# Accumulators of an input projection as tiles of one PSUM bank

## The chip, the cores and the metric

The kernel runs on one core of a Trainium2 chip. The metric is device time in microseconds of that core, from a whole execution. The engines are TensorE (PE in the profile, with PEld for its weight loads), VectorE (DVE), ScalarE (ACT), GpSimd (POOL) and SyncE (SP), whose queue issues most transfers. Each engine runs its own instructions in order and waits for the others by semaphores. TensorE adds its results up in PSUM, which this kernel uses as eight banks of 128 x 512 fp32.

## The reference

One encoder layer, applied with the same weights to two sequences of 512 tokens, D_MODEL = 1024, all fp32:

```python
h = rms_norm(x, norm_g)
proj = jnp.einsum('bsd,de->bse', h, w_in)
c_q, c_kv, k_rope, gate_a, conv_in, gate_c, mg_a, mg_c = split_columns(proj)
...                                     # latent attention with 8 heads
y_a = jnp.einsum('bse,ed->bsd', attn * jax.nn.silu(gate_a), w_o_attn)
u = conv_in[..., :CONV_WIDTH] * jax.nn.sigmoid(conv_in[..., CONV_WIDTH:])
...                                     # depthwise conv over 31 positions, + bias
u = jax.nn.silu(layer_norm(u, conv_ln_g, conv_ln_b)) * jax.nn.silu(gate_c)
y_c = jnp.einsum('bsc,cd->bsd', u, w_pw2)
merged = jax.nn.sigmoid(mg_a) * y_a + jax.nn.sigmoid(mg_c) * y_c
return x + jnp.einsum('bsd,de->bse', merged, w_out)
```

The change lies in `proj`, in those of its column blocks that feed the gates and the convolution, and in the LayerNorm and swish behind the convolution.

## The kernel before

Everything is computed channels first: a column block of the projection is 128 output channels by 1024 tokens (two sequences, "b" 0 and 1, of 512), that is two PSUM banks. Each fp32 matmul is made of three at higher pace: inputs and weights are split into a rounded part (hi) and the rest (lo), and hi\*hi, lo\*hi and hi\*lo are summed. ACT makes hi (L128 for plain weights, L178 for combined ones), POOL or DVE makes lo (L129, L179).

**The start.** The tokens are normalised and transposed on PE (`trans_x`, L275), read out of PSUM by ACT and DVE (`evac_x`, L306 and L307), and for the second sequence combined (`combine_x`, L290 to L299, with POOL). Meanwhile blk0 and blk1, the first two column blocks, are accumulated (L452, L461). blk0 is the gate half of the GLU's first pair (a "cb"), blk1 the value half ("ca").

**The streamed projection.** `plan` lists what follows: a *single* (L341) is one column block, 48 matmuls of 128x512 in the rows named blki (L325). A *seven* (L359) computes two column blocks together by a Strassen scheme with seven products instead of eight: each product (L351, matmuls at L355 to L357) is 12 matmuls into one bank. The seven's four banks are a and c, which are px (blkx in the profile), and d and b, which are py_ (blky). Its order on PE is a, b, d, b again, c, a again, d again, 84 matmuls. Between the products other engines work on the banks: ACT copies a (L372) and b (L375), POOL subtracts the copies (u2, L376), DVE makes v (L382), b = d - v (L383), c = c + v (L387) and d = d - u2 (L394). Combined weights for a seven come from sums on POOL (L147 to L158). There are 10 singles and 11 sevens from the first single (a cb) to the end of the last seven; twelve more singles follow, and the last six of them are the tail, in which `tokens` is interleaved.

**The readers.** `take` (L481) hands each finished pair of banks on: a cb goes through a sigmoid on ACT (L484), a ca is multiplied with it on DVE (u, L490), and gates go through an activation and to memory (`gate_out`, L476 and L477). From each u DVE computes the convolution, 30 taps of 128x1024 in a chain (L412), eight u's in all, each stored when done (y_s, L414). `drain` puts these taps between the products.

**Behind it.** `tokens` loads y back by tokens (L527), transposes it on PE (yT, L533), normalises it (L538 to L543), transposes again (zT, L549) and applies swish (L552 to L556), between the matmuls of the last singles. Then come the projection w_pw2 (`block`), attention, and w_out.

**PSUM.** Pool pp has three tiles of two banks [P, 2, S], for the column blocks, for px and py_, and for zT; p1 has two banks for x transposes, which py, the accumulator of the convolution, takes afterwards, and then yT. A matmul into a tile waits for an earlier reader or writer of the same tile.

**The order of the work.** PE's instructions in the projection stand in the order in which they are written (`manual_schedule`); the other engines' order is set ahead of time by a scheduler that goes by estimated times and the priorities given in the code. So an edit can move rows on engines that the text of the edit doesn't mention.

Of the kernel before, what the change touches and what calls it, by code (L numbers as in the profile page):

```python
# [9 lines left out]
F32 = mybir.dt.float32  # L10
# [33 lines left out]
def encoder_block(tc, xp_d, xs_d, win_d, wkr_d, whd_d, wqr_d, wo_d, wp_d, wout_d, vec_d, dwk_d, rg_d, rc_d, yp_d, ys_d):  # L44
# [275 lines left out]
    def block_mm(ps, i, xh, xl, grp, ks=range(KD)):  # L320
        whi, wlo = (w.rearrange("p (k c) -> p k c", k=KD) for w in wdone[i])
        for k in ks:
            for wl_, xl_, b in SEQ:
                if b in grp:
                    mm(  # L325
                        ps[:, b],
                        (wlo if wl_ else whi)[:, k],
                        xl(k, b) if xl_ else xh(k, b),
                        start=(k == 0 and wl_ == 0 and xl_ == 0),
                        stop=(k == KD - 1 and wl_ == 1),  # L330
                    )
# [6 lines left out]

    used = [0]

    def single(between=lambda: None):  # L341
        e = used[0]
        ensure(e + 3)
        ps = fresh(f"i{e}")
        block_mm(ps, stream[e][0], hh, hl, (0, 1), ks=range(4))
        between()
        block_mm(ps, stream[e][0], hh, hl, (0, 1), ks=range(4, KD))
        used[0] += 1
        return flat(ps)

# [8 lines left out]
    def seven(emit):  # L359

        e = used[0]
        px, py_ = fresh(f"x{e}"), fresh(f"y{e}")
        a, c, d, b = px[:, 0], px[:, 1], py_[:, 0], py_[:, 1]
        quad = lambda kk, bb: lambda k: (hH[4 * kk + k, bb], hL[4 * kk + k, bb])
# [25 lines left out]
        ensure(e + 6)  # L390
        emit(0, flat(px))
        product(d, e + 3, 0, comb(4), False)
# [3 lines left out]
        drain(3)  # L396
        emit(1, flat(py_))

# [67 lines left out]
    DVE.tensor_mul(gqk, vec[:, V_GQ : V_GQ + 1], vec[:, V_GK : V_GK + 1])  # L466
    close_pool("x", "p1")
    py = open_pool("py", bufs=1, space=PSUM)
# [4 lines left out]

    def gate_out(nm, j, pool, tag, ps):
        st = pool.tile([P, NT], F32, tag=tag, name=f"st{nm}{j}")
        ACT(st, ps, AF.Silu if nm[0] == "g" else AF.Sigmoid)  # L476
        nc.scalar.dma_start(spill[nm][j], st)  # L477

    sigs = {}

    def take(nm, j, ps):  # L481
        if nm == "cb":
            sigs[j] = cv.tile([P, NT], F32, tag="sig", name=f"sig{j}", bufs=1)
            ACT(sigs[j], ps, AF.Sigmoid)  # L484
        elif nm == "ca":
# [3 lines left out]
            with tc.high_priority(offset=100):  # L489
                DVE.tensor_mul(u[:, :, PAD : PAD + S], half(ps), half(sigs[j]))  # L490
            waiting.append(conv_ops(j, u))
        else:
            gate_out(nm, j, sp, "s", ps)

    take("cb", 0, flat(first[0]))
    take("ca", 0, flat(first[1]))
    with tc.manual_schedule(engines={nc.tensor.engine}):
# [48 lines left out]
    def swish(i, z):  # L546
        ps = pp.tile([P, KD, P], F32, tag="pp", name=f"zT{i}")
        for j in range(KD):
            nc.tensor.transpose(ps[:, j], z[:, j * P : (j + 1) * P], identf)  # L549
        zs = zp.tile([P, KD, P], F32, tag="zs", name=f"zs{i}")  # L550
        for j in range(KD):
            ACT(zs[:, j], ps[:, j], AF.Silu, scale=vec[:, V_LG + j : V_LG + j + 1], bias=vec[:, V_LB + j : V_LB + j + 1])  # L552
        DVE.tensor_mul(zs, zs, stok[i])
# [21 lines left out]
    for i in range(4):  # L575
        nc.gpsimd.tensor_mul(rt[:, i], rc[:, i % 2], rg[:, i].unsqueeze(1).to_broadcast([P, 4, RD]))
    close_pool("z", "s", "w1", "ln")
    wp = open_pool("w", bufs=2, side="left")
# [21 lines left out]
    close_pool("m", "c")  # L600
    p1 = open_pool("p1", bufs=2, space=PSUM)

# [528 lines left out]
```

## Time and profile before

| | |
|---|---|
| Median of 3 runs | 1210.38 us (1209.24 to 1213.36) |
| Profiled execution, its own time | 1211.43 us |
| Its span, first to last instruction | 1209.6 us |
| Mean granted TensorE clock | 0.994 |
| First matmul of a single (blki) between the x transposes | 29.87 us |
| First matmul of the first seven | 96.02 us |
| End of the last seven | 411.55 us |
| First transpose of `tokens` on PE | 487.71 us |

The profile names instructions by engine, source line, operation, and tile out<-in. A row of a timeline gives start and length in us, and in brackets how long the engine was idle ahead of it and what released it. Matmuls overlap, so that rows of 0.39 us follow each other at 0.23. A line of waits gives the engine and tile that waited, what it waited for, then total us, count, and the longest. SPq is SP issuing a transfer.

### The profile page before, as it was taken

The page shows a single profiled execution, that of the slowest core. Times are in us where ns is not written, and L with a number is a line of the kernel's source. Part 1 is how long each engine was busy: PE and PEld are TensorE (multiplying, and loading weights), DVE is VectorE, ACT ScalarE, POOL GpSimd, SP SyncE. Part 2 cuts the span into 40 slices and gives each one's busy share as a digit, 9 for nine tenths or more (in the row PEclk, how much of TensorE's full clock was granted, in tenths as well). Part 3 has the DMA queues.
Part 4 walks back from the last instruction along what each step waited for, and adds up shares of the span by engine and source line. Part 5 has one row for each costly group of instructions (what it writes and reads, how often), then busy time and mean ns, then how long its engine had stood idle before and what let it go on. Part 6 is the DMA issues. An engine that isn't in the chain of part 4 may idle for free.

```text
span 1209.6 us, 14998 instructions
## 1 busy us (share of the span) xinstructions
PE 1152.1 (95%) x5856; PEld 967.3 (80%) x5856; DVE 764.7 (63%) x1104; ACT 484.9 (40%) x871; POOL 343.4 (28%) x292
## 2 busy tenths in 40 slices
PE   7999989988988999999999999999999999999998
PEld 5677767767766788887888888799999998888887
DVE  5599999899999900573121345678778889343411
ACT  6532234233234221674011233766767687111200
POOL 5864565566466332210000001222221221000000
PEclk9999999999999999999999999999999999999999
DMA  6022212213213363453444011111001101234531
GB/s 248 1 71 87 87 53 106 87 53 105 87 53 114 130 204 105 132 152 117 157 156 139 28 47 60 62 34 34 25 19 34 33 30 39 85 132 160 186 105 70
DMA packets 46518, 109.51 MB, mean 91 GB/s; under 512 B 3696, under 2 KB 20336, under 8 KB 46448
## 3 DMA queue, kind: packets, MB, share of 16 engines
q1 hardware_dynamic: 41552, 91.78, 23.0%
q10 hardware_dynamic: 4896, 16.78, 3.6%
q8 instruction: 46, 0.75, 0.3%
q14 instruction: 24, 0.20, 0.0%
HBM read 79.18 MB, written 29.36 MB: 90 GB/s over the span
## 4 chain that ended last, share of the span: by engine, by line
PE 60%; DVE 5%; ACT 3%; issue 1%; POOL 1%; ACTq 0%; DVEq 0%; POOLq 0%
PE blk L325 21%; PE blki L325 8%; PE po L1053 7%; DVE py L412 3%; PE pt L820 2%; PE pkv L728 1%; PE pkv L730 1%; PE pkv L729 1%; PE av L830 1%; PE av L831 1%; PE av L832 1%; PE sc L801 1%; PE sc L803 1%; PE sc L802 1%; PE sc L804 1%
## 5 line engine op out<-in xcount | busy, mean ns | idle before, releaser
L412 DVE SCALAR_TENSOR_TENSOR py<-u,dwk,py 128x1024 f32<-128x1024 f32 x224 | 288.4, 1288 | 6.3
L128 ACT CAST whi<-raw 128x1024 fp32r<-128x1024 f32 (+3 forms) x59 | 60.5, 1025 | 300.9 <-PE blk L325 165.4
L325 PE MATMUL blki<-hH,whi 128*128 128x512 f32 x352 | 138.0, 392 | 1.7 <-ACT sig L484 1.7
L325 PE MATMUL blki<-hL,whi 128*128 128x512 f32 x352 | 137.1, 389 | 0.0
L325 PE MATMUL blki<-hH,wlo 128*128 128x512 f32 x352 | 108.5, 390 | 0.5 <-DVE wlo L129 0.5
L129 DVE TENSOR_TENSOR wlo<-raw,whi 128x1024 fp32r<-128x1024 f32 (+2 forms) x38 | 54.5, 1434 | 56.3 <-ACT whi L128 56.2
L355 PE MATMUL blky<-tH,ohi 128*128 128x512 f32 x176 | 69.8, 397 | 12.7 <-ACT u L375 12.7
L179 POOL TENSOR_TENSOR olo<-s,ohi 128x512 fp32r<-128x512 f32 x44 | 57.5, 1318 | 77.2 <-ACT ohi L178 77.2
L325 PEld LDWEIGHTS blki<-hH,whi 128*128 128x128 f32 x352 | 66.1, 188 | 15.6 <-ACT sig L484 2.1
L325 PEld LDWEIGHTS blki<-hH,wlo 128*128 128x128 f32 x352 | 66.0, 188 | 14.8 <-DVE wlo L129 0.9
L325 PEld LDWEIGHTS blki<-hL,whi 128*128 128x128 f32 x352 | 66.1, 188 | 13.4
L129 POOL TENSOR_TENSOR wlo<-raw,whi 128x1024 fp32r<-128x1024 f32 x20 | 48.2, 2412 | 82.5 <-ACT whi L128 82.5
L355 PE MATMUL blkx<-hH,ohi 128*128 128x512 f32 x132 | 54.1, 410 | 18.1 <-DVE blkx L387 18.1
L356 PE MATMUL blky<-tL,ohi 128*128 128x512 f32 x176 | 68.7, 390 | 0.0
L357 PE MATMUL blky<-tH,olo 128*128 128x512 f32 x176 | 68.5, 389 | 0.0
L325 PE MATMUL blk<-a,whi 128*128 128x512 f32 x256 | 68.4, 389 | 0.0
L178 ACT CAST ohi<-s 128x512 fp32r<-128x512 f32 x44 | 26.2, 619 | 103.7 <-PE blki L325 52.8
L811 ACT ACTIVATE pr<-sc,nm,sqs 128x512 f32<-128x512 f32 x64 | 51.1, 798 | 30.6 <-DVE nm L809 30.4
L251 POOL TENSOR_TENSOR rk<-sk,mhalf 128x4 f32<-128x4 f32 x16 | 17.2, 1074 | 146.6 <-DVE sk L738 146.6
L325 PE MATMUL blk<-hH,whi 128*128 128x512 f32 x144 | 57.5, 405 | 1.2 <-ACT hH L306 0.7
L325 PE MATMUL blk<-hL,whi 128*128 128x512 f32 x144 | 57.7, 401 | 0.2 <-DVE hL L307 0.2
L325 PEld LDWEIGHTS blk<-a,whi 128*128 128x128 f32 x256 | 48.0, 188 | 9.9
(254 smaller groups left out, 2930.3 us busy)
## 6 DMA issues: line engine op xcount, KB each, us to landing
raw<-in_win_dram SPq DMA_DIRECT2D x53, 512.0 KB, 3.6
y_s<-y SPq DMA_DIRECT2D x8, 512.0 KB, 2.6
ga_s<-stga ACTq DMA_DIRECT2D x8, 512.0 KB, 2.7
gc_s<-stgc ACTq DMA_DIRECT2D x8, 512.0 KB, 2.9
yt<-y_s SPq DMA_DIRECT2D x8, 512.0 KB, 5.1
gt<-gc_s SPq DMA_DIRECT2D x8, 512.0 KB, 4.2
mc_s<-stmc ACTq DMA_DIRECT2D x8, 512.0 KB, 3.0
raw<-in_wp_dram SPq DMA_DIRECT2D x8, 512.0 KB, 4.9
```

Of the source, the lines that this page charges most:

```text
L128: nc.scalar.copy(hv, rv)
L129: (sub or DVE).tensor_sub(lv, rv, f(hv))
L178: nc.scalar.copy(hi[:, sl], src)
L179: nc.gpsimd.tensor_sub(lo[:, sl], src, f(hi[:, sl]))
L325: mm(ps[:, b], (wlo if wl_ else whi)[:, k], xl(k, b) if xl_ else xh(k, b), start=(k == 0 and wl_ == 0 and xl_ == 0), stop=(k == KD - 1 and ...
L355: mm(ps, hi[:, k], xh, start=first and k == 0, stop=False, skip_group_check=not first)
L356: mm(ps, hi[:, k], xl, start=False, stop=False, skip_group_check=not first)
L357: mm(ps, lo[:, k], xh, start=False, stop=k == 3, skip_group_check=not first)
L412: DVE.scalar_tensor_tensor(out, u[:, :, i : i + S], dwk[:, j, i : i + 1], src, op0=ALU.mult, op1=ALU.add)
L811: ACT(pr, ps, AF.Exp, bias=nm, scale=r["sq"][:, j : j + 1], accum_out=sm)
L820: nc.tensor.transpose(pt[:, kt], pr[:, kt * P : (kt + 1) * P], identf)
L1053: mm(ps[:, n], lhs[k][:, ts_], w[k][:, n * S : (n + 1) * S], start=first_, stop=last_)
```

## The change

Each accumulator of the streamed projection becomes a tile of its own, of one bank [P, S], from a pool pb of six (banks 0 to 5), which takes the place of pp and p1 from the end of the start to the end of the tail. A single takes two such tiles, one for each sequence. A seven takes four, a, b, d and c. What `emit` and `take` are handed is a list of two tiles, and the sigmoid, the gates and the u multiplication are issued once per bank, on 128x512, where one instruction read 128x1024. zT takes two tiles as well. blk0 and blk1 stay pairs in pp. After the tail pb is closed, and pp and p1 are opened again.

```diff
--- before.py
+++ after.py
@@ -323,7 +323,7 @@
             for wl_, xl_, b in SEQ:
                 if b in grp:
                     mm(
-                        ps[:, b],
+                        ps[b] if isinstance(ps, list) else ps[:, b],
                         (wlo if wl_ else whi)[:, k],
                         xl(k, b) if xl_ else xh(k, b),
                         start=(k == 0 and wl_ == 0 and xl_ == 0),
@@ -337,16 +337,17 @@
         return flat(ps)
 
     used = [0]
+    one_bank = lambda name: pb.tile([P, S], F32, tag="pb", name=f"pb{name}")
 
     def single(between=lambda: None):
         e = used[0]
         ensure(e + 3)
-        ps = fresh(f"i{e}")
+        ps = [one_bank(f"i{e}_{b}") for b in range(2)]
         block_mm(ps, stream[e][0], hh, hl, (0, 1), ks=range(4))
         between()
         block_mm(ps, stream[e][0], hh, hl, (0, 1), ks=range(4, KD))
         used[0] += 1
-        return flat(ps)
+        return ps
 
     def product(ps, e, q, xs, first):
         hi, lo = (w[:, q * S : (q + 1) * S].rearrange("p (k c) -> p k c", k=4) for w in made[e])
@@ -359,8 +360,7 @@
     def seven(emit):
 
         e = used[0]
-        px, py_ = fresh(f"x{e}"), fresh(f"y{e}")
-        a, c, d, b = px[:, 0], px[:, 1], py_[:, 0], py_[:, 1]
+        a, b, d, c = (one_bank(f"{x}{e}") for x in "abdc")
         quad = lambda kk, bb: lambda k: (hH[4 * kk + k, bb], hL[4 * kk + k, bb])
         comb = lambda n: lambda k: (TH[n, k], TL[n, k])
         p_a = stp.tile([P, S], F32, tag="pa", name=f"pa{e}")
@@ -388,13 +388,13 @@
         drain(3)
         product(a, e + 2, 1, quad(1, 0), False)
         ensure(e + 6)
-        emit(0, flat(px))
+        emit(0, [a, c])
         product(d, e + 3, 0, comb(4), False)
         with tc.high_priority(offset=200):
             DVE.tensor_sub(d, d, u2)
         used[0] += 4
         drain(3)
-        emit(1, flat(py_))
+        emit(1, [d, b])
 
 
     y = {}
@@ -464,36 +464,40 @@
             nc.sync.dma_start(dwk, dwk_d)
     used[0] = 2
     DVE.tensor_mul(gqk, vec[:, V_GQ : V_GQ + 1], vec[:, V_GK : V_GK + 1])
-    close_pool("x", "p1")
+    close_pool("x", "p1", "pp")
+    pb = open_pool("pb", bufs=6, space=PSUM)
     py = open_pool("py", bufs=1, space=PSUM)
     sp = open_pool("s", bufs=2, side="left")
     cv = open_pool("cv", bufs=2, side="left")
     yp = open_pool("y", bufs=2, side="left")
     stp = open_pool("st", bufs=1, side="left")
 
-    def gate_out(nm, j, pool, tag, ps):
-        st = pool.tile([P, NT], F32, tag=tag, name=f"st{nm}{j}")
-        ACT(st, ps, AF.Silu if nm[0] == "g" else AF.Sigmoid)
-        nc.scalar.dma_start(spill[nm][j], st)
+    def gate_out(nm, j, ps):
+        st = sp.tile([P, 2, S], F32, tag="s", name=f"st{nm}{j}")
+        for b in range(2):
+            ACT(st[:, b], ps[b], AF.Silu if nm[0] == "g" else AF.Sigmoid)
+        nc.scalar.dma_start(spill[nm][j], flat(st))
 
     sigs = {}
 
     def take(nm, j, ps):
         if nm == "cb":
-            sigs[j] = cv.tile([P, NT], F32, tag="sig", name=f"sig{j}", bufs=1)
-            ACT(sigs[j], ps, AF.Sigmoid)
+            sigs[j] = cv.tile([P, 2, S], F32, tag="sig", name=f"sig{j}", bufs=1)
+            for b in range(2):
+                ACT(sigs[j][:, b], ps[b], AF.Sigmoid)
         elif nm == "ca":
             u = cv.tile([P, 2, UW], F32, tag="u", name=f"u{j}", bufs=3)
             nc.gpsimd.memset(u[:, :, 0:PAD], 0.0)
             nc.gpsimd.memset(u[:, :, PAD + S : UW], 0.0)
             with tc.high_priority(offset=100):
-                DVE.tensor_mul(u[:, :, PAD : PAD + S], half(ps), half(sigs[j]))
+                for b in range(2):
+                    DVE.tensor_mul(u[:, b, PAD : PAD + S], ps[b], sigs[j][:, b])
             waiting.append(conv_ops(j, u))
         else:
-            gate_out(nm, j, sp, "s", ps)
-
-    take("cb", 0, flat(first[0]))
-    take("ca", 0, flat(first[1]))
+            gate_out(nm, j, ps)
+
+    for nm, i in (("cb", 0), ("ca", 1)):
+        take(nm, 0, [first[i][:, b] for b in range(2)])
     with tc.manual_schedule(engines={nc.tensor.engine}):
         for u in plan[2 : len(plan) - NLN]:
             if isinstance(u[0], str):
@@ -544,12 +548,12 @@
         return z
 
     def swish(i, z):
-        ps = pp.tile([P, KD, P], F32, tag="pp", name=f"zT{i}")
+        ps = [one_bank(f"zT{i}_{q}").rearrange("p (j t) -> p j t", j=4) for q in range(2)]
         for j in range(KD):
-            nc.tensor.transpose(ps[:, j], z[:, j * P : (j + 1) * P], identf)
+            nc.tensor.transpose(ps[j // 4][:, j % 4], z[:, j * P : (j + 1) * P], identf)
         zs = zp.tile([P, KD, P], F32, tag="zs", name=f"zs{i}")
         for j in range(KD):
-            ACT(zs[:, j], ps[:, j], AF.Silu, scale=vec[:, V_LG + j : V_LG + j + 1], bias=vec[:, V_LB + j : V_LB + j + 1])
+            ACT(zs[:, j], ps[j // 4][:, j % 4], AF.Silu, scale=vec[:, V_LG + j : V_LG + j + 1], bias=vec[:, V_LB + j : V_LB + j + 1])
         DVE.tensor_mul(zs, zs, stok[i])
         sl = slice(i % 4 * P, (i % 4 + 1) * P)
         nc.scalar.copy(cH[i // 4][:, :, sl], zs)
@@ -574,7 +578,9 @@
             take(*u, single(lambda: tokens(2 * n + 1)))
     for i in range(4):
         nc.gpsimd.tensor_mul(rt[:, i], rc[:, i % 2], rg[:, i].unsqueeze(1).to_broadcast([P, 4, RD]))
-    close_pool("z", "s", "w1", "ln")
+    close_pool("z", "s", "w1", "ln", "pb")
+    pp = open_pool("pp", bufs=3, space=PSUM)
+    p1 = open_pool("p1", bufs=2, space=PSUM)
     wp = open_pool("w", bufs=2, side="left")
     nraw = 1
     prep(J["p", 0])
@@ -598,7 +604,6 @@
         nc.sync.dma_start(tc_s[j], t_)
         load_smc(j + 2)
     close_pool("m", "c")
-    p1 = open_pool("p1", bufs=2, space=PSUM)
 
 
     at = open_pool("at", bufs=1, side="left")
```

In the changed kernel the seven's lines up to `emit` keep their numbers, but product's matmuls are L356 to L358, sig is L487, gates L478 and the u multiplication L494.

**PE at the end of the start.** blk0 and blk1 are the pairs of the start, blki2 is the first single's pair, whi2 and wlo2 are its weights; names like DVE_49 are the semaphore of the engine waited for. Before:

```order
L325 MATMUL blk0_287<-hH0_1_355,whi0_180 128x512 [waits Activation_49]
L325 MATMUL blk1_312<-hH0_1_355,whi1_258 128x512
L325 MATMUL blki2_590<-hH0_1_355,whi2_523 128x512
L325 MATMUL blk0_287<-hL0_1_356,whi0_180 128x512 [waits DVE_49]
L325 MATMUL blk0_287<-hH0_1_355,wlo0_181 128x512
L325 MATMUL blk1_312<-hL0_1_356,whi1_258 128x512
L325 MATMUL blk1_312<-hH0_1_355,wlo1_259 128x512
L325 MATMUL blki2_590<-hL0_1_356,whi2_523 128x512
L325 MATMUL blki2_590<-hH0_0_216,wlo2_524 128x512
L325 MATMUL blki2_590<-hH0_1_355,wlo2_524 128x512
L325 MATMUL blki2_590<-hH1_0_220,whi2_523 128x512
L325 MATMUL blki2_590<-hL1_0_221,whi2_523 128x512
```

and now, with pbi2_0 and pbi2_1 as the first single's two banks:

```order
L325 MATMUL blk0_287<-hH0_1_355,whi0_180 128x512 [waits Activation_49]
L325 MATMUL blk1_312<-hH0_1_355,whi1_258 128x512
L325 MATMUL blk0_287<-hL0_1_356,whi0_180 128x512 [waits DVE_49]
L325 MATMUL blk0_287<-hH0_1_355,wlo0_181 128x512
...
L325 MATMUL blk1_312<-hH7_1_473,whi1_258 128x512
L325 MATMUL blk1_312<-hL7_1_474,whi1_258 128x512
L325 MATMUL blk1_312<-hH7_1_473,wlo1_259 128x512
L325 MATMUL pbi2_0_596<-hH0_0_216,whi2_523 128x512 [waits DVE_49]
L325 MATMUL pbi2_0_596<-hL0_0_217,whi2_523 128x512
L325 MATMUL pbi2_1_597<-hH0_1_355,whi2_523 128x512
L325 MATMUL pbi2_1_597<-hL0_1_356,whi2_523 128x512
L325 MATMUL pbi2_0_596<-hH0_0_216,wlo2_524 128x512
```

Before, 22 matmuls of the first single stand between those of blk0 and blk1. Now all of it stands behind the last matmul of blk1, and its first matmul has a wait for DVE, which is for the second half of the u0 multiplication, since pbi2_0 lies on a bank of blk1.

**PE in the first seven,** the first matmul of each product from b on (of the products in their order b, d, b, c, a, d). Before:

```order
L355 MATMUL blky6_864<-tH2_0_128,ohi6_0_718 128x512 [waits Activation_49]
...
L355 MATMUL blky6_864<-tH3_0_132,ohi6_1_792 128x512 [waits Activation_49]
...
L355 MATMUL blky6_864<-tH1_0_124,ohi6_1_792 128x512
...
L355 MATMUL blkx6_863<-hH4_1_359,ohi6_2_868 128x512
...
L355 MATMUL blkx6_863<-hH4_0_232,ohi6_2_868 128x512 [waits DVE_49]
...
L355 MATMUL blky6_864<-tH4_0_373,ohi6_3_903 128x512
```

and now, with a bank's letter in the name:

```order
L356 MATMUL pbb6_878<-tH2_0_128,ohi6_0_728 128x512 [waits DVE_49,Activation_49]
...
L356 MATMUL pbd6_879<-tH3_0_132,ohi6_1_804 128x512 [waits Activation_49]
...
L356 MATMUL pbb6_878<-tH1_0_124,ohi6_1_804 128x512 [waits Activation_49]
...
L356 MATMUL pbc6_880<-hH4_1_359,ohi6_2_884 128x512
...
L356 MATMUL pba6_877<-hH4_0_232,ohi6_2_884 128x512
...
L356 MATMUL pbd6_879<-tH4_0_373,ohi6_3_919 128x512 [waits DVE_49]
```

The wait for DVE has gone from a's second product and stands at d's second, where L383 has to be done; a wait for ACT, for the copy of b, is new at b's second product. The wait for ACT at d's first product (row two) stood for the weight's hi and for the copy of b; now it stands for the hi alone. The first product into b also waits for DVE now, for an earlier reader of its bank.

**DVE at the last seven:** v, d - v, c + v and d - u2, and the taps (L412) between and behind them, py7 being the accumulator of the eighth convolution block and py6 of the seventh. Before:

```order
L383 TENSOR_TENSOR blky52_2778<-blky52_2778,v52_2781 128x512 [waits DVE_49]
L412 SCALAR_TENSOR_TENSOR py7_2774<-u7_2461,dwk_80,py7_2774 128x1024 [waits DVE_49]
L387 TENSOR_TENSOR blkx52_2777<-blkx52_2777,v52_2781 128x512 [waits PE_49]
L412 SCALAR_TENSOR_TENSOR py7_2774<-u7_2461,dwk_80,py7_2774 128x1024 [waits DVE_49] x6
L394 TENSOR_TENSOR blky52_2778<-blky52_2778,u252_2780 128x512 [waits PE_49,Pool_49]
L412 SCALAR_TENSOR_TENSOR py7_2774<-u7_2461,dwk_80,py7_2774 128x1024 [waits DVE_49] x9
L412 SCALAR_TENSOR_TENSOR y7_2772<-u7_2461,dwk_80,py7_2774 128x1024 [waits DMAHW2_49,DVE_49]
L538 BN_STATS bst0_3380<-yT0_3371 128x6 [waits DMAHW1_49,PE_49]
```

and now:

```order
L383 TENSOR_TENSOR pbb52_2844<-pbd52_2845,v52_2849 128x512 [waits DVE_49]
L412 SCALAR_TENSOR_TENSOR py6_2526<-u6_2218,dwk_80,py6_2526 128x1024 [waits DVE_49]
L387 TENSOR_TENSOR pbc52_2846<-pbc52_2846,v52_2849 128x512 [waits PE_49]
L412 SCALAR_TENSOR_TENSOR py6_2526<-u6_2218,dwk_80,py6_2526 128x1024 [waits DVE_49] x3
L394 TENSOR_TENSOR pbd52_2845<-pbd52_2845,u252_2848 128x512 [waits PE_49,Pool_49]
L412 SCALAR_TENSOR_TENSOR py6_2526<-u6_2218,dwk_80,py6_2526 128x1024 [waits DVE_49] x5
L412 SCALAR_TENSOR_TENSOR y6_2524<-u6_2218,dwk_80,py6_2526 128x1024 [waits DMAHW6_49,DVE_49]
L412 SCALAR_TENSOR_TENSOR py7_2840<-u7_2518,dwk_80,y7_2838 128x1024 [waits DVE_49]
L412 SCALAR_TENSOR_TENSOR py7_2840<-u7_2518,dwk_80,py7_2840 128x1024 [waits DVE_49] x28
L412 SCALAR_TENSOR_TENSOR y7_2838<-u7_2518,dwk_80,py7_2840 128x1024 [waits DMAHW5_49,DVE_49]
L542 BN_STATS bst0_3464<-yT0_3455 128x6 [waits DMAHW2_49,PE_49]
```

Behind d - u2 (L394) there were 10 taps; now there are 36, of which 30 are the whole of the eighth block.

## The prediction

> **What bounds the kernel now.** I read the page first, then the waits of PE over the input projection, then the rows of one seven, then the two ends of that stage, because an edit of accumulators can only save time where PE waits for the reader of an accumulator.
>
> ```profile
> PE 1152.1 (95%) x5856; PEld 967.3 (80%) x5856; DVE 764.7 (63%) x1104; ACT 484.9 (40%) x871; POOL 343.4 (28%) x292
> ...
> PE blk L325 21%; PE blki L325 8%; PE po L1053 7%; DVE py L412 3%; PE pt L820 2%; PE pkv L728 1%; PE pkv L730 1%; PE pkv L729 1%; PE av L830 1%; PE av L831 1%; PE av L832 1%; PE sc L801 1%; PE sc L803 1%; PE sc L802 1%; PE sc L804 1%
> 411.71 76.17 PE blki L325 x336
> ```
>
> PE is busy for 95% of the span, so little is to be had elsewhere. The third line is a step of the chain of waits (start, length, what): 336 matmuls of 128x512 without one wait, 76.17/336 = 0.2267 us each. That is the full pace, and everything in the streamed projection is made of it: a product (12 matmuls) is 2.72 us, a seven (84) 19.04, a single (48) 10.88.
>
> Next come the waits of PE from 60 to 450 us, and busy time of each engine from 65.4 to 411.5 us (columns: length, then busy us and count of PE, weight loads, DVE, ACT, POOL):
>
> ```profile
> PE blkx L355 <- DVE blkx L387: 18.1, 11, 2.4
> PE blky L355 <- ACT u L375: 12.7, 11, 1.8
> PE blki L325 <- ACT sig L484: 1.7, 1, 1.7
> PE blki L325 <- DVE wlo L129: 0.5, 1, 0.5
> 65.40:411.50 346.10, 315.26 (x1348) 253.40 (x1347) 327.60 (x280) 112.50 (x151) 192.58 (x153) 0.99 0.25 84
> ```
>
> Eleven sevens, two waits in each, and practically nothing else. Both come from a tile of two banks: product d waits until ACT has copied b (L375), which shares py_ with it, and the second product of a waits until DVE has added v to c (L387), which shares px. One seven at full length:
>
> ```profile
> 96.02 0.39 PE L355 MATMUL blkx<-hH,ohi 128*128 128x512 f32 x1
> ...
> 101.23 0.39 PE L357 MATMUL blky<-tH,olo 128*128 128x512 f32 x1
> 102.63 0.50 PE L355 MATMUL blky<-tH,ohi 128*128 128x512 f32 x1 [1.01 <-ACT u L375]
> ...
> 110.74 0.39 PE L357 MATMUL blkx<-hH,olo 128*128 128x512 f32 x1
> 111.92 0.50 PE L355 MATMUL blkx<-hH,ohi 128*128 128x512 f32 x1 [0.79 <-DVE blkx L387]
> ...
> 117.50 0.39 PE L325 MATMUL blki<-hH,whi 128*128 128x512 f32 x1
> ```
>
> It lasts 117.50 - 96.02 = 21.48 us, 2.44 more than 19.04, of which the two rows name 1.01 + 0.79 = 1.80. So each stall costs about 0.32 us more than its row says, since PE drains and refills. The longest wait of all, 2.36 us, costs more still:
>
> ```profile
> 404.39 0.79 PE L355 MATMUL blkx<-hH,ohi 128*128 128x512 f32 x1 [2.36 <-DVE blkx L387]
> 404.98 0.63 PE L356 MATMUL blkx<-hL,ohi 128*128 128x512 f32 x1
> ...
> 407.88 0.39 PE L357 MATMUL blkx<-hH,olo 128*128 128x512 f32 x1
> ...
> 411.55 0.39 PE L325 MATMUL blki<-hH,whi 128*128 128x512 f32 x1
> ```
>
> Behind it eight matmuls take 407.88 - 404.39 = 3.49 us instead of 1.81: the clock was at half, 1.7 us lost. The last seven ends at 411.55, where the long chain step begins.
>
> **The change, gain first.** With one bank to a tile, the second product of a waits for nothing (c + v lies in another tile), and d waits only for its weights. New waits stand in their place: b's second product waits for ACT's copy of b, with the 2.72 us of product d between, where ACT was late by 1.4 (101.23 to 102.63); d's second product waits for L383 (b = d - v), with two products, 5.44 us, between. On DVE L382 and L383 stand with a tap between them:
>
> ```profile
> 108.52 0.69 DVE L382 TENSOR_TENSOR v<-pa,blky 128x512 f32<-128x512 f32 x1 [0.41 <-PE blky L357]
> 109.12 1.27 DVE L412 SCALAR_TENSOR_TENSOR y<-u,dwk,py 128x1024 f32<-128x1024 f32 x1
> 110.31 0.69 DVE L383 TENSOR_TENSOR blky<-blky,v 128x512 f32<-128x512 f32 x1
> ```
>
> v began 0.3 us after the last matmul into b (108.25 by the pace), and L383 ended at 111.0, so 2.75 us after b was full. Against 5.44 that leaves some **2.7 us of margin**, as long as v starts at once.
>
> What the stalls cost in all follows from the ends, and from the rows of the start (PE, DVE, ACT and POOL in turn; the last line is DVE's group of the weight splits over the whole span):
>
> ```profile
> 54.49 0.39 PE L325 MATMUL blk<-hH,wlo 128*128 128x512 f32 x1
> ...
> 62.49 0.50 PE L325 MATMUL blki<-hH,whi 128*128 128x512 f32 x1 [1.72 <-ACT sig L484]
> 55.32 8.77 DVE L129 TENSOR_TENSOR wlo<-raw,whi 128x1024 fp32r<-128x1024 f32 x1 [1.36 <-ACT whi L128]
> 64.02 1.21 DVE L490 TENSOR_TENSOR u<-blk,sig 128x1024 f32<-128x1024 f32 x1
> 61.41 1.02 ACT L484 ACTIVATE sig<-blk 128x1024 f32<-128x1024 f32 x1
> 59.40 2.38 POOL L129 TENSOR_TENSOR wlo<-raw,whi 128x1024 fp32r<-128x1024 f32 x1
> 61.74 1.28 POOL L299 TENSOR_TENSOR tL<-t,tH 128x512 fp32r<-128x512 f32 x1
> 63.33 1.92 POOL L299 TENSOR_TENSOR tL<-t,tH 128x512 fp32r<-128x512 f32 x1
> L129 DVE TENSOR_TENSOR wlo<-raw,whi 128x1024 fp32r<-128x1024 f32 (+2 forms) x38 | 54.5, 1434 | 56.3 <-ACT whi L128 56.2
> ```
>
> The second single begins at 62.49. From there to the end of the last seven lie 9 singles and 11 sevens, 1356 matmuls or 307.4 us, and they took 411.55 - 62.49 = 349.1. So 41.7 us are lost: 30.8 in the two waits, 22 x 0.32 = 7.0 in refills, 0.5 for wlo, and the rest, 3.4, is two dips of the clock of 1.7. The change takes nearly all of it away: **-41.7 us**.
>
> **What it costs.** The first single (blki2) had a slot of its own in pp, so PE put 22 of its matmuls between the x transposes and the rest right behind blk0 and blk1, from about 54.7 on. Now its first bank is the one in which blk1 (the first ca) lies, and it waits until DVE has multiplied the second half of u0. In the trace u0 is DVE's row at 64.02, behind a wlo that took 8.77 us, where the other 37 of its group mean (54.5 - 8.8)/37 = 1.2. It ended at 64.1, just when POOL, back to back since 59.40 at least, came to a short gap between its rows of 61.74 and 63.33; that DVE was held up by POOL is my reading. Two halves of about 0.65 each end at 65.3, so the first single begins at about **65.4**. Against before that is 65.4 - 62.49 = 2.9 us later and a whole single, 10.9 us, more to do: **+13.8**. PE idles 11 us ahead of it (54.5 to 65.4) and starts at half clock; the dip behind 2.36 us cost 1.7, and I take **+2.0** with the refill.
>
> *A rule on this:* the Trainium skill, "TensorE: Matmul & The Clock Gate", section "Part 1: The HAM clock gate", says that an idle window of about 3.4 us throttles PE to half and about 3.4 us of work releases it; by it the new hole costs about 1.7 us and the 2.36 us wait should have cost nothing. The rows at 404.98 show half pace after the shorter wait, with the same 3.5 us to recover, so I keep the trace's price.
>
> For the start I see two bounds. If less filling on PE lets the x phase end earlier by all of its 22 matmuls (5.0 us), it is 60.4; if POOL leaves no gap and wlo waits for two more of its operations (2.4 + 1.3), it is about 69. POOL's rows run back to back whatever PE does, so I stay near the trace's own.
>
> Then 1404 x 0.2267 = 318.3 us: 65.4 + 2.0 + 318.3 = 385.7. I add 0.9 for small stalls (a hundredth of a us per product is not excluded), **386.6** against 411.55, or -25.0.
>
> **Does DVE keep up?** It has 327.6 us of work in a stretch of 346.1, and now the stretch is 321 (65.4 to 386.6). Behind it come the end of the convolution, its store and load (SP's queue, and the time to land of the load), and the tokens that want it:
>
> ```profile
> 412.06 0.69 DVE L394 TENSOR_TENSOR blky<-blky,u 128x512 f32<-128x512 f32 x1
> 412.66 11.88 DVE L412 SCALAR_TENSOR_TENSOR py<-u,dwk,py 128x1024 f32<-128x1024 f32 x9
> 424.57 1.28 DVE L412 SCALAR_TENSOR_TENSOR y<-u,dwk,py 128x1024 f32<-128x1024 f32 x1
> 426.15 0.42 SPq L414 DMA_DIRECT2D y_s<-y  x1
> 431.70 0.38 SPq L527 DMA_DIRECT2D yt<-y_s  x1
> yt<-y_s SPq DMA_DIRECT2D x8, 512.0 KB, 5.1
> DVE bst L538 <- PE yT L533: 62.9, 1, 62.9
> 487.71 1.04 PE L533 MATMUL yT<-identf,yt 128*128 128x128 f32 x8
> ```
>
> What gives is the taps of the convolution (L412, 1.32 us each): by DVE's new order 36 of them stand behind the last L394 where 10 stood. They move 26 x 1.32 = 34 us of work behind the last seven, so DVE's 327.6 becomes about 293 + 3 us of gates in halves, and some 20 us of slack are left over 11 sevens. The last seven at 386.6, L394 at about 388.5, 36 x 1.32 = 47.5: the convolution ends at about 436. The store and the turn to the load took 431.70 - 424.57 = 7.1 us, landing 5.1: yt is there at about 448. PE wants it at 487.71 - 25 = 462.7, so 14 us of DVE's 62.9 us pause remain as cover. If the cover went, each us beyond it would be paid.
>
> **Small terms.** Two groups of the page size them, a copy of one bank on ACT and a split on POOL:
>
> ```profile
> L372 ACT COPY pa<-blkx 128x512 f32<-128x512 f32 x11 | 6.5, 586 | 8.9 <-PE blkx L357 7.7 <-ACT stgc L476 1.2
> L179 POOL TENSOR_TENSOR olo<-s,ohi 128x512 fp32r<-128x512 f32 x44 | 57.5, 1318 | 77.2 <-ACT ohi L178 77.2
> ```
>
> ACT issues 45 more rows and DVE 12, all halves of a reader of both banks. A half costs 0.59 on ACT, so two take 0.16 more than one of both banks (1.02, the sig row), off PE's path as the gates have a product's time at least; in the tail, where gates and tokens lie on the chain, 3 or 4 of them give about **+0.5**. POOL has 12 operations of some 1.3 per seven, 15.8 us of 19.04, so weights come in time, if narrowly. Closing six banks and opening the pairs falls behind the tail, where the first block takes banks that the last single doesn't hold: 0.
>
> **Sum.** -41.7 + 13.8 + 2.0 + 0.9 + 0.5 = **-24.5 us**. The profiled execution took 1211.43 (span 1209.6 and 1.8 around it), the median is 1210.38; -24.5 from each gives 1186.9 and **1186**.
>
> **Rivals.**
> 1. *DVE becomes the bound.* For it: 95% busy in the window. Against: 34 us of taps move out. If v starts late behind a tap or two and d's second product waits 1.2 us (one tap) in each seven, 11 x (1.2 + 0.3) = 16 us return: 1202. Chance 0.06.
> 2. *The start costs more.* First single at 69 or 70: 1191. Within the main case's range; 0.12. By the same measure an earlier start gives 1181.
> 3. *Weights come late: slower than before.* PE now asks for four halves each 19.04 us instead of 21.5, POOL needs 15.8, and sums, splits and loads hang in one chain of ACT and POOL. From 2.2 us per seven (24.5/11) the gain is gone; at 2.6 with refill it ends at 1214. The trace has no wait of a seven for olo or whi in eleven, which speaks against; 0.04.
> 4. *The waits stay.* Were the banks still tracked by pair, only the losses remain, 13.8 + 2.0 + 0.5: 1226. The new order shows no wait at a's second product; 0.02.
> 5. *Nothing is left.* The same lateness at 1.9 us per seven, 11 x (1.9 + 0.3) = 24, leaves 1210; 0.04.
>
> The forecast itself with 1181 to 1192 has 0.72 (with the second rival 0.84). From the same cases: faster by over 0.3% (3.6 us, about what a measurement of this kernel can tell) 0.90, within it 0.04, slower 0.06. To hold 8 in 10 with part of the first rival I take 1180 to 1197.
>
> **What would show it.** In the new profile PE's waits on L387 and L375 should be gone (right) or stand under the new names with 10 us or more (wrong: first rival). The first matmul of pbi2 should stand at 64 to 66, with half pace for 3.5 us and the u multiplication ahead of it. The last seven should end at 384 to 389 and the long run of singles begin there. 36 taps should follow the last L394, the last ending before 440, and the first yT at about 463 without a wait. I am wrong if PE waits for a tap-bound DVE in every seven, if wlo holds u0 beyond 69, or if the tail after 463 takes over 1 us more than it did.

## The result

The median is 1183.59 us over four runs (1183.32 to 1184.55), against 1211.87 us for the kernel before over four runs. The ratio is 0.9767, with a 95% interval of 0.9741 to 0.9794, so the change made the kernel 2.3% faster. The forecast was 1186 us. The profiled execution took 1184.55 us with a span of 1182.8, against 1211.43 and 1209.6 before: 26.8 us of span.

PE's waits from 50 to 450 us, in the changed kernel, are this one line (engine and tile, what was waited for, then total us, count, longest):

```profile
PE pbi L325 <- DVE u L494: 8.1, 1, 8.1
```

Before there were four lines, two of them with eleven waits each. None of the 22 is left. The same shows in busy time from the first single to the end of the last seven (length, then busy us and count of PE, weight loads, DVE, ACT, POOL):

```profile
64.88:385.24 320.36, 320.36 (x1404) 265.22 (x1405) 295.10 (x261) 116.79 (x177) 192.62 (x153) 0.99 0.26 89
```

PE is busy in 320.36 of 320.36 us, and DVE has 295.10 us of work in the stretch, where before it had 327.60 in 346.10. The first seven and the end of the last on PE:

```profile
110.52 0.39 PE L356 MATMUL pba<-hH,ohi 128*128 128x512 f32 x1
...
126.84 0.39 PE L356 MATMUL pbd<-tH,ohi 128*128 128x512 f32 x1
...
129.56 0.39 PE L325 MATMUL pbi<-hH,whi 128*128 128x512 f32 x1
...
385.24 0.39 PE L325 MATMUL pbi<-hH,whi 128*128 128x512 f32 x1
```

A seven is 129.56 - 110.52 = 19.04 us, where it was 21.48: to the hundredth the 84 matmuls at full pace. The row at 126.84 is d's second product, which now has the wait for L383. The last seven ends at 385.24 instead of 411.55. At the start, on PE, DVE and POOL:

```profile
56.39 0.39 PE L325 MATMUL blk<-hH,wlo 128*128 128x512 f32 x1
64.88 0.80 PE L325 MATMUL pbi<-hH,whi 128*128 128x512 f32 x1 [8.11 <-DVE u L494]
65.47 0.63 PE L325 MATMUL pbi<-hL,whi 128*128 128x512 f32 x1
...
69.71 0.39 PE L325 MATMUL pbi<-hH,whi 128*128 128x512 f32 x1
56.54 7.09 DVE L129 TENSOR_TENSOR wlo<-raw,whi 128x1024 fp32r<-128x1024 f32 x1 [2.96 <-ACT whi L128]
63.55 1.28 DVE L494 TENSOR_TENSOR u<-blk,sig 128x512 f32<-128x512 f32 x2
61.28 1.26 POOL L299 TENSOR_TENSOR tL<-t,tH 128x512 fp32r<-128x512 f32 x1
62.86 1.90 POOL L299 TENSOR_TENSOR tL<-t,tH 128x512 fp32r<-128x512 f32 x1
```

The first single stands behind u0, and u0 behind a weight split of 7.09 us; PE starts at half pace. And the end of the convolution on DVE, its way back through memory on SP, and the tokens on PE; below it the group of the loads (the last number is us to landing):

```profile
432.48 1.28 DVE L412 SCALAR_TENSOR_TENSOR y<-u,dwk,py 128x1024 f32<-128x1024 f32 x1
438.08 0.38 SPq L531 DMA_DIRECT2D yt<-y_s  x1
461.40 1.03 PE L537 MATMUL yT<-identf,yt 128*128 128x128 f32 x8
```

```profile
yt<-y_s SPq DMA_DIRECT2D x8, 512.0 KB, 5.3
```

The convolution ends 7.9 us later than before, at 433.8 (432.48 + 1.28, against 424.57 + 1.28), and yt lands at about 443.4. PE asks for it at 461.40 and doesn't wait.

### The profile page after: what moved, and what is told of

The parts are those of the page before. It is cut to its first block, busy times and chain, and to the rows that moved or that the text cites. A ratio compares the mean times of both kernels' runs of the same rounds, so it can differ in the third digit from the quotient of the medians.

```text
span 1182.8 us, 15035 instructions
## 1 busy us (share of the span) xinstructions
PE 1145.4 (97%) x5856; PEld 969.4 (82%) x5856; DVE 763.1 (65%) x1112; ACT 488.5 (41%) x909; POOL 343.3 (29%) x292
## 4 chain that ended last, share of the span: by engine, by line
PE 92%; POOL 3%; ACT 3%; DVE 1%; issue 1%; DMA 1%; SPq 0%; ACTq 0%; DVEq 0%
PE blk L325 22%; PE pbi L325 20%; PE po L1058 7%; PE pt L825 2%; PE pbd L356 2%; PE pba L356 2%; PE pbb L356 2%; PE pbd L358 2%; PE pba L358 2%; PE pbb L358 2%; PE pbb L357 2%; PE pbd L357 2%; PE pba L357 2%; PE pkv L733 1%; PE pkv L735 1%; PE pkv L734 1%
## 5 line engine op out<-in xcount | busy, mean ns | idle before, releaser
L412 DVE SCALAR_TENSOR_TENSOR py<-u,dwk,py 128x1024 f32<-128x1024 f32 x224 | 288.5, 1288 | 6.2
L325 PE MATMUL pbi<-hH,whi 128*128 128x512 f32 x352 | 138.9, 395 | 8.1 <-DVE u L494 8.1
L325 PE MATMUL pbi<-hL,whi 128*128 128x512 f32 x352 | 137.9, 392 | 0.0
L325 PE MATMUL pbi<-hH,wlo 128*128 128x512 f32 x352 | 108.9, 391 | 0.0
L325 PEld LDWEIGHTS pbi<-hH,whi 128*128 128x128 f32 x352 | 66.6, 189 | 22.1 <-DVE u L494 8.5
L325 PEld LDWEIGHTS pbi<-hH,wlo 128*128 128x128 f32 x352 | 66.5, 189 | 14.0
L325 PEld LDWEIGHTS pbi<-hL,whi 128*128 128x128 f32 x352 | 66.7, 190 | 13.6
L179 POOL TENSOR_TENSOR olo<-raw,ohi 128x512 fp32r<-128x512 f32 x33 | 43.7, 1324 | 35.2 <-ACT ohi L178 26.5
L325 PE MATMUL blk<-cH,whi 128*128 128x512 f32 x128 | 50.7, 396 | 2.4 <-ACT whi L128 2.4
L1061 DVE TENSOR_TENSOR o<-po,xr 128x1024 f32<-128x1024 f32 (+1 forms) x9 | 10.0, 1106 | 64.2 <-PE po L1058 64.2
L603 DVE TENSOR_TENSOR tmc<-blk,smc 128x1024 f32<-128x1024 f32 x8 | 9.8, 1225 | 64.2 <-PE blk L325 64.2
```

Of the source, the lines that this page charges most:

```text
L179: nc.gpsimd.tensor_sub(lo[:, sl], src, f(hi[:, sl]))
L325: mm(ps[b] if isinstance(ps, list) else ps[:, b], (wlo if wl_ else whi)[:, k], xl(k, b) if xl_ else xh(k, b), start=(k == 0 and wl_ == 0 a ...
L412: DVE.scalar_tensor_tensor(out, u[:, :, i : i + S], dwk[:, j, i : i + 1], src, op0=ALU.mult, op1=ALU.add)
```

## Experiments

Where a kernel was timed several times, an interval is given. The others have one time and one trace, and there I read the places in the trace rather than the total.

**The readers alone.** The kernel before, with its pairs of banks, and each reader split in two:

```diff
-        ACT(st, ps, AF.Silu if nm[0] == "g" else AF.Sigmoid)
+        for b in range(2):
+            ACT(half(st)[:, b], half(ps)[:, b], AF.Silu if nm[0] == "g" else AF.Sigmoid)
```

and likewise the sigmoid and the u multiplication.

> The kernel before, with its pairs of banks, but the sigmoid, the gates and the u multiplication issued once per bank. Theory (the gain is the two waits inside a seven, which come from a reader of one bank holding the other bank of its tile): the readers have no part in it, PE's waits on L375 and L387 stay at 11 each and about 31 us in all, the time stays at 1208 to 1214 us. Rival (the readers in halves are what makes room): a good part of the 28 us appears, 1185 to 1200 us, and the waits shrink below 15 us.

Measured: 1209.38 us, ratio 0.9984 (0.9973 to 0.9996). PE's waits:

```profile
PE blkx L355 <- DVE blkx L387: 15.8, 11, 2.3
PE blky L355 <- ACT u L375: 11.7, 11, 1.3
```

All 22 waits stand, 27.5 us where there were 30.8. Halving the readers is not what the change lives on; the 2 us are too little to explain.

**a and c in one tile again.** The change, with

```diff
-    pb = open_pool("pb", bufs=6, space=PSUM)
+    pb = open_pool("pb", bufs=4, space=PSUM)
+    pq = open_pool("pq", bufs=1, space=PSUM)
...
-        a, b, d, c = (one_bank(f"{x}{e}") for x in "abdc")
+        px = pq.tile([P, 2, S], F32, tag="pq", name=f"px{e}")
+        a, c = px[:, 0], px[:, 1]
+        b, d = (one_bank(f"{x}{e}") for x in "bd")
```

> The change, but a and c of a seven share a tile of two banks again (one such tile, and four single banks for the rest). Theory (the two waits are separate costs): PE waits on L387 at a's second product come back, 11 of about 1.65 us with 0.3 us refill each and one or two dips of the clock, 1204 to 1209 us. Rival (the two waits share one cause, DVE's pace, so that taking one away only lengthens the other): the whole 40 us come back, 1220 us or more, or nothing comes back.

**d and b in one tile again,** the same with d and b in the pair:

> The change, but d and b of a seven share a tile of two banks again (one such tile, and four single banks for the rest). Theory: PE waits on ACT's copy of b (L375) at d's first product come back, 11 of about 1.15 us with 0.3 us refill each, 1198 to 1202 us. Rival (DVE's pace is behind both): nothing comes back, 1183 to 1187 us.

Measured: 1214.83 us and 1205.13 us, both above the expected ranges. PE's waits up to 530 us, of the first and then of the second:

```profile
PE px L356 <- DVE px L389: 16.1, 11, 1.7
PE pbi L325 <- DVE u L497: 9.1, 1, 9.1
PE px L356 <- ACT stgc L481: 2.2, 3, 0.7
PE px L356 <- ACT sig L490: 2.0, 3, 0.7
```

```profile
PE py L356 <- ACT u L377: 11.1, 11, 1.0
PE pbi L325 <- DVE u L497: 9.5, 1, 9.5
PE py L356 <- ACT pa L374: 1.8, 3, 0.6
```

Each pair brings back its own eleven waits, the ones that the kernel before has, and not the other's. The last seven ends at 410.6 with a and c together and at 402.3 with d and b together, against 385.2. The first singles of the three traces don't start alike (63.99, 64.60, 64.88), so I take the eleven sevens alone: they last 25.6 and 17.1 us longer in all than in the change. With 0.32 us of refill for each of 17 and of 14 waits, the lines make 20.3 + 5.4 = 25.7 and 12.9 + 4.5 = 17.4. So the price per wait, the row plus some 0.3, holds. Of the 25.6, 6.1 belong to the pair having only one tile in turn (the six waits for stgc and sig), which the kernel before doesn't have. What is lost beyond the sevens lies in the tail, where the transposes and the singles now share four banks: from the end of the last seven to the first block behind the tail the two runs take 153.3 and 153.2 us, the change 148.3. The next run, with four banks too, takes 153.2. So the two waits are separate costs: 16.1 + 11.1 = 27.2 us here, 30.8 where both stand.

**Four banks instead of six.** The change with `bufs=4`, all else as it is.

> The change with a pool of four one-bank tiles in place of six. Theory (both the one-bank grain and two banks beyond a seven's four are needed): the unit behind a seven takes the banks of a and b at once, b is read last, behind d - u2 and the readers, so PE waits 1.5 to 2.5 us in most of the 11 sevens' wakes, and the tail, whose transposes take two banks as well, loses 3 to 5 us: 1198 to 1212 us. Rival (the grain alone is what counts): the projection keeps its pace, only the tail loses, 1186 to 1190 us.

Measured: 1188.07 us, the rival's number. PE's waits up to 530 us:

```profile
PE pbi L325 <- DVE u L494: 9.2, 1, 9.2
PE pbi L325 <- ACT stmc L478: 4.6, 4, 1.8
```

The first single starts at 65.67 and the last seven ends at 386.54, 320.9 us, within 0.5 us of the change (half clock at the start lasts 1.05 us longer here, to 70.98, which makes that difference). The 4.6 us are four waits in the tail, and most of their price is paid: up to the first block behind the tail it takes 539.73 - 386.54 = 153.2 us, against 148.3. The whole stretch behind the last seven is only 2.2 us longer (1186.3 - 386.54 = 799.8 us, against 797.6), since the change's trace has two stretches at half clock there, at 533 and 735 us, and this one has none. I had expected the next unit to wait for b's bank. It doesn't, so in the projection the grain of one bank does the work and the two spare banks do nothing; the tail alone uses them.

**Two products exchanged,** so that d's second comes before a's second:

```diff
-        product(a, e + 2, 1, quad(1, 0), False)
-        ensure(e + 6)
-        emit(0, [a, c])
         product(d, e + 3, 0, comb(4), False)
         with tc.high_priority(offset=200):
             DVE.tensor_sub(d, d, u2)
+        ensure(e + 6)
+        product(a, e + 2, 1, quad(1, 0), False)
+        emit(0, [a, c])
```

> The change with the last two products of a seven exchanged, so that d's second product comes 2.72 us behind b's second (with product c between) instead of 5.44 us. Theory (L383 ends some 2.75 us after b is full, a margin of 2.7 us as the change stands): d's second product now waits for L383 in most sevens, 0.1 to 0.6 us each with 0.3 us refill, 1187 to 1194 us. Rival (DVE runs later than that, and the margin is nearly used up): 1 us or more in each seven, 1198 us or more; or DVE is early enough, no wait and 1183 us.

Measured: 1187.05 us, at the low edge. PE's waits for L383:

```profile
PE pbd L356 <- DVE pbb L383: 0.3, 1, 0.3
```

One wait only, and yet the stretch from the first single (65.29) to the end of the last seven (389.2) is 323.9 us, 3.5 more than 320.36. Of this 3.3 lie in the sevens, which take 19.27 to 19.65 us instead of 19.04, 0.3 us more each. That is the refill without a wait to speak of: L383 is ready just when PE gets there. With 2.72 us less between, the margin is about zero, so with the order of the change it is 2.7 us, as worked out.

**The weight split ahead of u0,** on POOL in place of DVE:

```diff
-                    split(i, nc.gpsimd if i >= 4 else None)
+                    split(i, nc.gpsimd if i >= 3 else None)
```

> The change with one weight split (wlo3, which took DVE 7.1 us from 56.5 to 63.6 ahead of u0) on POOL in place of DVE. Theory (DVE was held up by POOL, and u0 stood behind it): u0 runs as soon as its sigmoid is there, at about 62.1, the first single begins at 63.3 to 63.6 instead of 64.88, the split takes POOL some 2.4 us, and the kernel ends 1 to 1.5 us earlier if POOL's queue doesn't take it back: 1181 to 1184 us. Rival (u0 waits for the sigmoid or the end of blk1 anyway): the first single stays at 64.5 to 65.

Measured: 1181.29 us, 2.3 less than the change's median; in the trace the last seven ends 2.1 us earlier, at 383.17. PE, then DVE, then POOL:

```profile
63.38 0.80 PE L325 MATMUL pbi<-hH,whi 128*128 128x512 f32 x1 [7.69 <-DVE u L494]
62.04 1.29 DVE L494 TENSOR_TENSOR u<-blk,sig 128x512 f32<-128x512 f32 x2 [7.98 <-ACT sig L487]
66.67 7.55 DVE L412 SCALAR_TENSOR_TENSOR py<-u,dwk,y 128x1024 f32<-128x1024 f32 x1 [3.34 <-ACT y L406]
59.38 4.68 POOL L129 TENSOR_TENSOR wlo<-raw,whi 128x1024 fp32r<-128x1024 f32 x2
```

u0 runs when its sigmoid is there, and the first single starts 1.5 us earlier and is back at full clock after 3.0 us instead of 4.3. On POOL the two splits take 2.34 each, where DVE was at one for 7.09. Now the first tap, which reads u and y, takes 7.55 us beside a busy POOL, and PE doesn't wait for it.

**The first single's banks.** The one-bank pool from the start, so that the x transposes and blk0 and blk1 use it as well:

```diff
-    pp = open_pool("pp", bufs=3, space=PSUM)
+    pb = open_pool("pb", bufs=6, space=PSUM)
...
-        pair = pp.tile([P, 2, S], F32, tag="pp", name=f"xT0_{i}")
-        banks[i], banks[i + 2] = pair[:, 0], pair[:, 1]
+        banks[i], banks[i + 2] = one_bank(f"xT0_{i}"), one_bank(f"xT0_{i + 2}")
...
-        first[i] = fresh(i)
+        first[i] = [one_bank(f"blk{i}_{b}") for b in range(2)]
...
-    close_pool("x", "p1", "pp")
-    pb = open_pool("pb", bufs=6, space=PSUM)
+    close_pool("x", "p1")
```

> The change, but the pool of six one-bank tiles is there from the start, so that the x transposes and blk0 and blk1 are single banks of it too and the first single finds banks 2 and 3 free. Theory (the start of the change lost one single of 10.9 us, 2.4 us of a later start and 2.1 us of half clock): the first single is again put between the x transposes, the second begins at about 62.5 us, the last seven ends near 371 instead of 385.2, and the kernel takes 1168 to 1172 us. The convolution still ends near 433 us, as DVE waited only some 20 us in the stretch. Rival (DVE has no more to give): PE waits in the sevens for L383 or at the first token transpose for the convolution, and 5 us or less is gained, 1178 to 1184 us.

Measured: 1171.44 us over four runs, ratio 0.9666 to the kernel before (0.9651 to 0.9680). On PE the second single and the end of the last seven; then all of PE's waits from 60 to 450 us:

```profile
61.23 0.50 PE L327 MATMUL pbi<-hH,whi 128*128 128x512 f32 x1 [1.35 <-ACT sig L486]
...
369.92 0.39 PE L327 MATMUL pbi<-hH,whi 128*128 128x512 f32 x1
```

```profile
PE pbi L327 <- ACT sig L486: 1.4, 1, 1.4
PE pbi L327 <- DVE wlo L129: 0.9, 1, 0.9
PE yT L536 <- DMA yt<-y_s: 0.6, 1, 0.6
```

The first single again lies between the x transposes, and no start at half clock is left. The last seven ends 15.3 us earlier than in the change, the span is 14.6 us shorter, and the median 12.2 us lower. So the loss at the start was the size that the sum gave it, and it wasn't a necessary part of the change. This version beats both kernels. Its third line shows the next limit: the convolution ends at 431.7, and PE already waits 0.6 us for yt.

**More work for DVE.** The change with idle additions behind c = c + v, first eight and then three in each seven:

```diff
             DVE.tensor_add(c, c, v)
+            for _ in range(8):
+                DVE.tensor_add(v, v, v)
```

> The change with eight more DVE operations of 128x512 in each seven (v = v + v behind c + v, when v is dead; about 0.5 to 0.6 us each, 44 to 53 us in all). Theory (DVE has some 16 us of waits in the stretch and the tokens some 18 us of cover, and more work only puts taps behind the last seven): PE waits little in the sevens, the convolution ends at 460 to 470 us instead of 433.8, and PE waits 8 to 20 us for yt at the first token transpose, 1191 to 1205 us. Rival (more DVE work holds up v and d - v in every seven): PE waits 15 us or more on L383 and on the readers, ahead of the last seven's end, and the end of the last seven moves from 385 to 400 us or more.

Measured with eight: 1227.52 us, far beyond the expected range. The load, and PE's waits up to 530 us:

```profile
L389 DVE TENSOR_TENSOR v<-v 128x512 f32<-128x512 f32 x88 | 85.4, 971 | 0.0
```

```profile
PE yT L539 <- DMA yt<-y_s: 17.4, 1, 17.4
PE pbd L356 <- DVE pbb L383: 15.7, 7, 4.2
PE pbi L325 <- DVE u L496: 9.6, 1, 9.6
```

The load was 85 us and not 44 to 53, since one addition took 0.97 us on average, so this run does not tell the theories apart: PE waits in both places, and the last seven ends at 411.1. That DVE can hold up d - v in the sevens when it has far too much to do is shown by it, as my first rival had it. With three:

> The change with three more DVE operations of 128x512 in each seven, 33 in all, where the run before this had 88, which took 0.97 us each (85.4 us), some up to 2.6. Theory (DVE has some 16 us of waits to give in the stretch and 18 us of cover behind it): 33 x 0.97 = 32 us of work, 16 of them absorbed, the convolution ends at 446 to 452 us instead of 433.8, yt comes in time or 1 us late, PE waits less than 4 us in the sevens: 1184 to 1190 us. Rival (each us of DVE work is paid on PE): PE waits on L383 in most sevens, the last seven ends beyond 395, 1195 us or more.

Measured: 1185.52 us. PE's waits up to 480 us:

```profile
PE pbi L325 <- DVE u L496: 8.8, 1, 8.8
PE yT L539 <- DMA yt<-y_s: 2.1, 1, 2.1
```

The additions took 35.5 us by their rows, 3 more than expected. No seven waits; the last one ends at 385.44, the convolution at 453.3, 19.5 us later than in the change and 1.3 beyond the expected range, and PE waits 2.1 us at the tokens. Since rows overlap a little, DVE's busy time up to the end of the convolution rises by 31.3 us. Of these, 12.4 lie ahead of the end of the last seven, where DVE's idle time falls from 25.3 to 13.7 us, and 18.9 behind it. Of the 19.5 us by which the convolution ends later, 17.4 were covered. What was only argued before, that DVE's surplus is taken up by its idle time and by the cover behind the last seven, and not by PE in the sevens, holds up to this load.

## Why the prediction was right

| Term of the sum | forecast, us | measured, us |
|---|---|---|
| Waits inside the sevens | -41.7 | -41.7 |
| First single later and not filled in | +13.8 | +13.3 |
| Start at half clock | +2.0 | +2.1 |
| Small stalls | +0.9 | 0 |
| Tail | +0.5 | -0.5 |
| Sum | -24.5 | -26.8 |

The first measured term is what the kernel before lost, all of which is gone, since each of the eleven sevens takes 19.04 us now. The others are 64.88 - 62.49 + 10.88 = 13.3 for the start; 320.36 - 1404 x 0.2267 = 2.1 for the clock and everything else up to the last seven; and (1182.8 - 385.24) - (1209.6 - 411.55) = -0.5 behind it.

- *The waits.* All went, refills and dips of the clock with them, and nothing took their place. The price of 0.32 us beyond a wait's row, taken from one seven, came out again, at 0.30 to 0.31, in both pair runs and in the run with two products exchanged.
- *New waits.* b's second product and d's second never waited. The margin of 2.7 us at d was right by the run that took 2.72 away, and by the rows of the last seven in the change: L383 ends at 379.84, and d's second product begins at 382.52.
- *The start.* 65.4 was forecast, 64.88 measured, by the mechanism named: u0 behind a split that POOL held up. In the seven traces that have this start unchanged the first single begins between 63.99 and 65.67. That half clock came out at 2.1 us is in part luck: in the same seven traces it lasts 4.3 to 6.2 us from the first matmul, which costs 2.1 to 3.1. The x phase did not end earlier for having 22 matmuls less; blk1's last matmul came at 56.39, later than in the kernel before, as PE ran at half pace in parts of the phase (its matmuls stand 0.43 us apart from 49.4 to 52.0).
- *DVE.* It kept up. Of the stretch it was idle 320.36 - 295.10 = 25.3 us, 19.6 of them in listed waits. The forecast said some 20 us of slack, but its own numbers, 293 + 3 of 321 us, leave 25. The cover was 18 us where 14 were forecast: the 36 taps ended at 433.8 (forecast 436), the load was issued 4.3 us behind that, and the forecast had added 7.1 us, counted from the start of the last tap, to its end, 1.3 too much.
- *The two terms that missed.* The 0.9 us for small stalls were not there: a seven is 19.04 us exactly. The tail was given +0.5 for halves that cost ACT more; it came out at -0.5. (The halves are also fewer than the forecast's 45 and 12: by the profiles' pages ACT has 909 rows instead of 871, 38 more, and DVE 1112 instead of 1104, 8 more.) On ACT, before and in the change, the last gate:

```profile
556.64 1.28 ACT L476 ACT_TABLE_LOAD   x1
557.93 1.02 ACT L476 ACTIVATE stmc<-blki 128x1024 f32<-128x1024 f32 x1
```

```profile
527.67 1.28 ACT L478 ACT_TABLE_LOAD   x1
530.88 1.09 ACT L478 ACTIVATE stmc<-pbi 128x512 f32<-128x512 f32 x2 [1.92 <-PE pbi L325]
```

  Its two halves take 1.09 against 1.02, but ACT was ahead of PE this time, and the gate ended 1.5 us behind the last row of matmuls (530.45) instead of 1.9 (557.03). Two halves cost 0.07 more here and not the 0.16 of the forecast. What brought ACT ahead wasn't tried by itself.
- *The rivals.* Weights never came late: no wait for olo or whi in a seven, at 192.6 us of POOL in 320.4. The waits went and no seven is late, so the fourth and the fifth are out. The second, a first single at 69 or 70, didn't come in any of the seven traces. The first, DVE as the bound, is real, but 35.5 us of added rows brought no wait in a seven, and 85.4 us brought seven.

## What to carry to other kernels

A tile that spans two banks makes every reader of one bank a lock on the other, and the listed wait is only part of the price: here each cost some 0.3 us more, and two of the longest a stretch at half clock. When the allocation of accumulators changes, look at where the first new tile lands: here it landed on a bank still being read, which took back 15 of the 42 us gained, and a pool that was there from the start gave 12 us of them back. Before adding buffers, try the grain alone: four banks did in the projection what six did.

## What was not expected of the hardware

*The clock.* Short waits could cost PE its full pace, and it wasn't the length of a wait alone that decided. The first block behind the tail, in the change:

```profile
533.51 0.80 PE L325 MATMUL blk<-cH,whi 128*128 128x512 f32 x1 [2.45 <-ACT whi L128]
534.11 0.63 PE L325 MATMUL blk<-cL,whi 128*128 128x512 f32 x1
...
536.95 0.39 PE L325 MATMUL blk<-cH,whi 128*128 128x512 f32 x1
```

A wait of 2.45 us gave 3.4 us of half pace, as 2.36 us did twice before the change. But a wait of 2.41 us in the kernel before cost nothing of the kind:

```profile
381.35 0.50 PE L355 MATMUL blkx<-hH,ohi 128*128 128x512 f32 x1 [2.41 <-DVE blkx L387]
381.69 0.40 PE L356 MATMUL blkx<-hL,ohi 128*128 128x512 f32 x1
```

And in five of the other traces (four banks, the split on POOL, d and b in one tile, three and eight additions) the same block behind the tail comes after the same 2.45 us and runs at full pace. What tells them apart is a grid: within each trace, all the moments at which the granted clock changes lie whole multiples of 3.41 us apart. Of the kernel before, four cells of that grid (length, PE's busy time and count, then the other engines; the third number from the end is the granted clock):

```profile
288.28:291.69 3.41, 1.05 (x5) 0.56 (x4) 3.41 (x5) 0.00 (x0) 1.14 (x1) 1.00 0.36 78
291.70:295.11 3.41, 3.41 (x10) 2.64 (x9) 3.34 (x3) 0.00 (x0) 2.13 (x2) 0.50 0.39 160
377.03:380.44 3.41, 1.90 (x9) 1.25 (x7) 3.41 (x5) 0.18 (x1) 3.31 (x3) 1.00 0.00 0
380.45:383.86 3.41, 2.52 (x11) 2.06 (x12) 3.34 (x5) 0.00 (x0) 0.00 (x0) 1.00 0.00 0
```

The first wait of 2.36 us (288.77 to 291.14) lies in one cell, and the next cell runs at half clock; the wait of 2.41 us (378.93 to 381.35) falls on two cells, and neither has a half-clock cell behind it. From 60 to 560 us of all eleven traces, 13 cells at full clock hold 1.83 us or more of PE's idle time, and each is followed by half clock; the other 1549 cells at full clock hold 1.72 us at most, and none of them is. So for waits of about 2.4 us it is their place on the grid that decides, and an edit that moves one can gain or lose 1.7 us by chance. This also sets the price at the first single, where half clock lasts until a cell ends: 4.3 us, from 64.88 to 69.14, at a cost of 2.1 us.

The Trainium skill, "TensorE: Matmul & The Clock Gate", section "Part 1: The HAM clock gate (the "warmup" mystery)", has about 3.4 us of idleness as the window after which the clock is halved, and about the same to get it back. The time to get it back agrees, at 3.41 us. The idle time doesn't: here 1.83 us of it within one cell were enough.

*DVE beside POOL.* A weight split on DVE, 1.2 us by its group, took 7 to 9 us when POOL was busy without a gap, and so did the first tap (7.55 us), both with two inputs from SBUF; the additions v + v took 0.68 to 2.6. The Trainium skill, "SBUF — State Buffer", section "Who interferes with whom", says that a DVE instruction with both inputs in SBUF contends with a GpSimd instruction that reads SBUF; by its section "Summary: rules for kernel authors" the one that issues second blocks until the first has finished. The rows agree, and go further: in the change DVE's split didn't get its turn between two POOL instructions. It ended at 63.63, 1.1 us after POOL had come to a few memsets at 62.5 us, and POOL's next row, at 62.86, took 1.90 us instead of 1.26. The 224 taps whose second input is py, in PSUM, took 1.29 us on average.
